# Handover from layer 0 to attention: last squares, row order of the first projection, evacuation, weight and key transfers

## The chip, the cores and the metric

The kernel runs on one core of one Trainium2 chip. The time is the device time of one execution in microseconds, and the figure for a kernel is the median of its runs. Before the change it is 2207.64 us (three runs, 2205.65 to 2208.02).

## What is computed

A trunk of two layers for one sequence of 1024 positions with 1024 features, all in float32. Layer 0 is a gated linear recurrence with a SwiGLU block behind it, layer 1 is stick-breaking attention (16 heads of 64) with a SwiGLU block of 2816 hidden features behind it; each block is normalised before and added to its input after. The change touches the end of layer 0's SwiGLU block and the attention:

```python
def swiglu_ffn(x, w_in, w_out):
    gu = jnp.einsum("bsd,df->bsf", x, w_in)
    h = jax.nn.silu(gu[..., :D_FF]) * gu[..., D_FF:]
    return jnp.einsum("bsf,fd->bsd", h, w_out)

# attention, per block of 128 queries
z = jnp.einsum("bhqd,bhkd->bhqk", qb, kb) * scale
log_fail = jnp.where(strict, jax.nn.log_sigmoid(-z), 0.0)
suffix = lax.cumsum(log_fail, axis=3, reverse=True) - log_fail
weights = jnp.where(strict, jnp.exp(jax.nn.log_sigmoid(z) + suffix), 0.0)
o = jnp.einsum("bhqk,bhkd->bhqd", weights, vb)      # then o @ w_o

# layers
h = h + mixer(rms_norm(h, mix_norm[layer]))
h = h + swiglu_ffn(rms_norm(h, ffn_norm[layer]), w_in, w_out)
```

## The kernel before

**Numbers and tiles.** Each float32 operand of a product is kept as two parts, a high part in a rounded format and the rest. A product is three matmuls, high by high, high by low, low by high (`mm3`, lines 140 to 143). Activations lie with features on partitions: `h[d][n]`, `xh[d][n]`, `xl[d][n]` for 8 feature tiles `d` and two halves `n` of 512 positions; `xh` and `xl` are the two parts of the next block's input (the trace names their memory `vh`, `vl` or `xg`). The norm's factor per position is applied behind a product: squares of the rows of `h` are summed in `rbc[n]`, `stats` (line 201) sums over partitions on PE, `rstd` (176 to 183) makes the factor on ACT and DVE, `broadcast_r` (189, 196) writes it back into `rbc[n]` over all partitions.

**The end of layer 0.** `mix_out_ffn_in` runs a SwiGLU block as seven products for eight (sums of weight and activation tiles, written to `wah`, `wal`, `wbh` and so on by ACT and DVE at lines 640 to 690). Its last part goes over 13 visits to pairs of output tiles (`VISITS`). When an output tile is final, `finished(d, n)` (1035) stores `h` on SP's queue, prepares `xh` on ACT (215) and `xl` on DVE (216), squares the tile on ACT (211) and adds the square to `rbc[n]` on DVE (212). The last two visits end the tiles 0, 3, 4 and 7.

**Attention.** `qkv_steps(q)` is a generator for the projections of one pair of heads `q` of eight. For queries, keys and values (`which` 0, 1, 2; one of these is called a link) and each half `n` it accumulates eight `mm3` into one of the two buffers of psQ, one per step, so a link has 16 steps. Behind the eighth, in the same step, it evacuates: DVE multiplies by `rbc[n]` into `t` (1337); for queries and keys ACT casts the high part (1346), DVE subtracts the low part (1347), and SP moves the parts to their places with four DMAs for queries and eight of 128 KB for keys (1348). Values go through four transposes on PE (1362) into another psQ buffer, a cast on ACT (1366) and a subtraction on DVE (1367) for each head; this is put off (`late`) until the fourth step of the next half, or to the end. The list `later` holds the low parts of the next link's weights (1309); their high part is one ACT cast at the start of the link (1307), which also asks for the raw weights (512 KB, three buffers).

**The order in attention** is written by hand for PE, ACT, DVE and POOL; a scheduler places SP's DMAs. First come 32 steps of the first pair, queries and keys, with the two statistics and broadcasts between them. Then one iteration per unit `u` from -8 to 191 (a head has 12 units): the scores of unit `u+8` (`z_part`, 1388 and 1389), transposes and split of the weights of unit `u+2` (`t_part` 1426, `t_split` 1435 and 1436), the rest of `u+8` (two sigmoids on ACT 1408 and 1409, a scan on DVE 1412 or 1414, a multiplication on POOL 1415), one item of `later`, two steps of `all_fill`, and the products with the values of unit `u` (`av_part`, 1447 and 1448). Outputs of finished heads are gathered and split (1457 to 1467), and most of them are stored to DRAM (`od`).

**The end of the projections.** `all_fill` takes the steps of all pairs, brings the stored outputs back into `xh` and `xl` with 26 DMAs of 256 KB (1495, 1496), waits two steps, transposes the last values, closes psQ, splits a weight of the output projection (168, 169), opens the PSUM tile `ob` in psQ's banks, waits two steps, and then does 14 `mm3` of the output projection into `ob`, one per unit.

Of the kernel before, what the change touches and what calls it, by code (L numbers as in the profile page):

```python
# [16 lines left out]
P = 128  # L17
S = 1024
# [15 lines left out]
def trunk(  # L34
# [92 lines left out]
    def cols(w, c0, n=P):  # L127
        return w[:, c0 : c0 + n].rearrange("(k p) c -> p k c", p=P)
# [468 lines left out]
    def mix_out_ffn_in(h, mix, bias, layer, gnext, ob):  # L597
# [124 lines left out]
        with tc.manual_schedule(engines={E.PE, E.Activation, E.DVE, E.Pool}):  # L722
# [309 lines left out]
            begun_sq = set()  # L1032
# [252 lines left out]
    with ExitStack() as st:  # L1285
# [11 lines left out]
        Q, KH, KL, VV = {}, {}, {}, {}  # L1297
# [5 lines left out]
        late, later = [], []  # L1303
# [11 lines left out]
        def qkv_steps(q):  # L1315
            full = lambda tag: [ap.tile([P, S], F32R, tag=tag, name=tag, bufs=4) for _ in range(2)]
            VV[q] = ap.tile([P, NT, 2, P], F32R, tag="v", name="v", bufs=2)
            for which in range(3):
                w = wq.pop((q, which))
                nx = (q, which + 1) if which < 2 else (q + 1, 0)  # L1320
                if nx[0] < NP:
                    wq[nx] = next_weights(load_raw(cols(w_qkv, nx[1] * D + nx[0] * P), (ND,)))
                else:
                    mix[0].load(0)
                    mix[0].w[mix[0].order[0]] = next_weights(mix[0].raw.pop(0))
                    mix[0].load(1)
                    mix[0].load(2)
                for n in range(NH):
                    ps = psQ.tile([P, NB], F32, tag="qk", name="qk_ps")
                    for k in range(ND):  # L1330
                        mm3(ps, w[0][:, k], w[1][:, k], xh[k][n], xl[k][n], k == 0, k == ND - 1)
                        if k == 3 and late:
                            late.pop()()
                        if k < ND - 1:
                            yield
                    t = ap.tile([P, NB], F32, tag="t", name="t", bufs=2)
                    nc.vector.tensor_mul(t, ps, rbc[n])
                    cs = slice(n * NB, (n + 1) * NB)
                    if which == 0 and n == 0:
                        Q[q] = full("q")  # L1340
                    if which == 1 and n == 0:
                        KH[q], KL[q] = full("kh"), full("kl")
                    if which < 2:
                        th = ap.tile([P, NB], F32R, tag="qh_", name="qh_", bufs=1)
                        tl = ap.tile([P, NB], F32R, tag="ql_", name="ql_", bufs=1)
                        nc.scalar.copy(th, t)
                        nc.vector.tensor_sub(tl, t, f32(th))
                        move = lambda dst, p0, src, p1: nc.sync.dma_start(f32(dst)[p0, cs], f32(src)[p1])
                        for hx, (a, b) in enumerate(((top, bot), (bot, top))):
                            if which == 0:  # L1350
                                move(Q[q][hx], a, th, a)
                                move(Q[q][hx], b, tl, a)
                            else:
                                for dst, src in ((KH[q][hx], th), (KL[q][hx], tl)):
                                    move(dst, top, src, a)
                                    move(dst, bot, src, a)
                    else:

                        def v_turn(n=n, t=t):
                            tp = psQ.tile([P, NB], F32, tag="qk", name="vt_ps")  # L1360
                            for i in range(4):
                                nc.tensor.transpose(tp[:, i * P : (i + 1) * P], t[:, i * P : (i + 1) * P], ident)
                            src = tp.rearrange("p (b h c) -> p b h c", b=4, h=2)
                            bs = slice(4 * n, 4 * n + 4)
                            for hx in range(2):
                                nc.scalar.copy(VV[q][:, bs, hx, 0:HD], src[:, :, hx])
                                nc.vector.tensor_sub(
                                    VV[q][:, bs, hx, HD:P], src[:, :, hx], f32(VV[q])[:, bs, hx, 0:HD]
                                )

                        late.append(v_turn)
                    yield
# [11 lines left out]
        def z_part(q, hx, j, ci, c0, c1, diag):  # L1384
            nk = (j + 1) * P
            ps = psZ.tile([P, NB], F32, tag="z", name="z_ps")
            lhsT = Q[q][hx][:, j * P : (j + 1) * P]
            nc.tensor.matmul(ps[:, 0 : c1 - c0], lhsT=lhsT, rhs=KH[q][hx][:, c0:c1], start=True, stop=False)  # L1388
            nc.tensor.matmul(ps[:, 0 : c1 - c0], lhsT=lhsT, rhs=KL[q][hx][:, c0:c1], start=False, stop=True)  # L1389
            return ps  # L1390
# [90 lines left out]

        def stats_steps():
            for n in range(NH):
                stats(rbc[n], psO, "o", n)
                for _ in range(ND - (1 if n else 6)):
                    yield
                broadcast_r(psO, "o", n)
                yield

        def all_fill():  # L1490
# [14 lines left out]
            for _ in range(2):  # L1505
                yield
# [85 lines left out]
```

## Time and profile before

| what | value |
|---|---|
| median of the runs | 2207.64 us |
| profiled execution | 2209.81 us |
| its span, first to last instruction | 2207.9 us |
| mean granted clock of PE | 0.994 |
| busy share of PE, DVE, ACT, POOL | 99%, 77%, 52%, 13% |
| layer 0 ends, projections begin | about 964 us |
| first scores, last projections | 994.3 us, 1431.6 us |

The profile gives the busy time of each engine, groups of instructions by line, the waits of an engine (how long it was idle before a line's instruction, and which instruction on which engine ended the idle time), and rows of single instructions: start, duration, engine, line, operation, what is written from what, and in brackets the idle time ahead of it with its releaser. Rows of a stretch give its limits, its length, the busy time of PE, of PE's weight load, DVE, ACT and POOL with their counts, the granted clock, and the share of the DMA engines. A clock under 1.00 makes the matmuls of the stretch longer, and the longer matmuls count as busy. Two matmuls overlap: the distance between their starts is what one costs.

### The profile page before, as it was taken

What the parts mean: (1) busy time and instruction counts of PE and PEld (TensorE: products, weight loads), DVE (VectorE), ACT (ScalarE), POOL (GpSimd) and SP (SyncE); (2) the same over time, 40 slices, a digit from 0 to 9 for tenths busy, and PEclk for the clock granted to TensorE, in tenths of its full rate; (3) what the DMA queues carried; (4) which work ended last, traced back from release to release, by engine and by line L of the source; (5) the groups of instructions that cost most, each with busy time, mean ns of one, the idle gap of its engine ahead of it and who ended that gap; (6) DMA issues with size and microseconds to landing.
All of it is one profiled execution on the core that took longest, in us unless ns stands there. A gap on an engine that the chain in (4) does not pass through costs nothing.

```text
span 2207.9 us, 28478 instructions
## 1 busy us (share of the span) xinstructions
PE 2176.5 (99%) x10120; PEld 1805.7 (82%) x10120; DVE 1709.9 (77%) x2383; ACT 1150.2 (52%) x2007; POOL 287.2 (13%) x379
## 2 busy tenths in 40 slices
PE   7999999999999999999999999989999999999998
PEld 6888888888888888878888888878888888888887
DVE  6887778767777887878888888876876777788876
ACT  5577435343444544546666666653533444454556
POOL 2222020000000000003334333321000000000002
PEclk9999999999999999999999999989999999999999
DMA  7111412334444764444333333532133444467442
GB/s 230 48 48 39 134 39 72 102 123 158 143 149 134 261 209 122 148 136 98 89 94 96 105 87 104 177 128 70 39 110 124 148 148 133 154 225 234 137 152 86
DMA packets 298702, 277.72 MB, mean 126 GB/s; under 512 B 16312, under 2 KB 215104, under 8 KB 298560
## 3 DMA queue, kind: packets, MB, share of 16 engines
q1 hardware_dynamic: 298544, 275.91, 40.1%
q8 instruction: 79, 1.29, 0.2%
q14 instruction: 63, 0.52, 0.1%
q10 hardware_dynamic: 16, 0.00, 0.0%
HBM read 175.71 MB, written 74.97 MB: 114 GB/s over the span
## 4 chain that ended last, share of the span: by engine, by line
PE 88%; DVE 6%; ACT 3%; DMA 1%; issue 1%; SPq 1%; DVEq 0%; ACTq 0%
PE p_ps L143 18%; PE p_ps L141 18%; PE p_ps L142 18%; PE qk_ps L143 3%; PE qk_ps L141 3%; PE qk_ps L142 3%; PE wt_ps L1426 3%; PE ob_ps L142 2%; PE ob_ps L141 2%; PE ob_ps L143 2%; PE a_ps L143 2%; PE a_ps L142 2%; PE a_ps L141 2%; PE z_ps L1388 1%; DVE F L1414 1%; PE z_ps L1389 1%
## 5 line engine op out<-in xcount | busy, mean ns | idle before, releaser
L1415 POOL TENSOR_TENSOR w<-w,F 128x128 f32<-128x128 f32 (+1 forms) x192 | 183.7, 957 | 311.1 <-DVE F L1412 159.0
L143 PE MATMUL p_ps<-vh,wcl 128*128 128x512 f32 x524 | 204.2, 390 | 0.5 <-DVE wcl L682 0.5
L143 PE MATMUL p_ps<-vh,wbl 128*128 128x512 f32 x524 | 204.4, 390 | 0.3 <-DVE wbl L672 0.2
L143 PE MATMUL p_ps<-vh,wal 128*128 128x512 f32 x524 | 204.1, 389 | 0.1
L141 PE MATMUL p_ps<-vh,wbh 128*128 128x512 f32 x524 | 204.2, 390 | 0.0
L141 PE MATMUL p_ps<-vh,wch 128*128 128x512 f32 x524 | 204.1, 389 | 0.0
L142 PE MATMUL p_ps<-vl,wbh 128*128 128x512 f32 x524 | 203.9, 389 | 0.0
L142 PE MATMUL p_ps<-vl,wch 128*128 128x512 f32 x524 | 203.9, 389 | 0.0
L141 PE MATMUL p_ps<-vh,wah 128*128 128x512 f32 x524 | 203.9, 389 | 0.0
L142 PE MATMUL p_ps<-vl,wah 128*128 128x512 f32 x524 | 203.9, 389 | 0.0
L668 ACT CAST wbh<-sb 128x1024 fp32r<-128x1024 f32 (+2 forms) x69 | 69.6, 1009 | 193.7 <-DVE sb L652 193.6
L212 POOL TENSOR_TENSOR acc<-acc,rbc 128x512 f32<-128x512 f32 x30 | 40.4, 1348 | 773.6 <-ACT rbc L211 773.6
L1436 DVE TENSOR_TENSOR tl<-wt_ps,th 128x512 fp32r<-128x512 f32 x192 | 106.0, 552 | 39.2 <-ACT th L1435 37.1
L1435 ACT CAST th<-wt_ps 128x512 fp32r<-128x512 f32 x192 | 92.5, 482 | 83.1 <-PE wt_ps L1426 82.0
L141 PE MATMUL qk_ps<-vh,whi 128*128 128x512 f32 x264 | 118.6, 449 | 0.7 <-ACT vh L215 0.7
L143 PEld LDWEIGHTS p_ps<-vh,wbl 128*128 128x128 f32 x524 | 98.3, 188 | 22.3 <-DVE wbl L672 2.0
L143 PEld LDWEIGHTS p_ps<-vh,wcl 128*128 128x128 f32 x524 | 98.4, 188 | 21.9 <-DVE wcl L682 1.6
L143 PEld LDWEIGHTS p_ps<-vh,wal 128*128 128x128 f32 x524 | 98.4, 188 | 21.3 <-DVE wal L663 1.0
L142 PEld LDWEIGHTS p_ps<-vl,wah 128*128 128x128 f32 x524 | 98.4, 188 | 20.6
L142 PEld LDWEIGHTS p_ps<-vl,wch 128*128 128x128 f32 x524 | 98.4, 188 | 20.5
L142 PEld LDWEIGHTS p_ps<-vl,wbh 128*128 128x128 f32 x524 | 98.4, 188 | 20.5
L141 PEld LDWEIGHTS p_ps<-vh,wbh 128*128 128x128 f32 x524 | 98.4, 188 | 20.3 <-ACT ta L1053 0.2
(400 smaller groups left out, 5851.2 us busy)
## 6 DMA issues: line engine op xcount, KB each, us to landing
raw<-in_ffn_w_in SPq DMA_DIRECT2D x88, 512.0 KB, 3.8
vl<-pd SPq DMA_DIRECT2D x128, 256.0 KB, 3.6
pd<-U SPq DMA_DIRECT2D x90, 256.0 KB, 2.3
raw<-in_ffn_w_out SPq DMA_DIRECT2D x56, 256.0 KB, 3.9
raw<-in_attn_w_qkv SPq DMA_DIRECT2D x24, 512.0 KB, 3.8
raw<-in_lru_w_in SPq DMA_DIRECT2D x16, 512.0 KB, 4.1
acc<-pd SPq DMA_DIRECT2D x28, 256.0 KB, 2.6
pph<-rbc SPq DMA_DIRECT2D x28, 256.0 KB, 2.5
```

The source lines that it names most:

```text
L141: nc.tensor.matmul(ps, lhsT=wh, rhs=mh, start=first, stop=False, **kw)
L142: nc.tensor.matmul(ps, lhsT=wh, rhs=ml, start=False, stop=False, **kw)
L143: nc.tensor.matmul(ps, lhsT=wl, rhs=mh, start=False, stop=last, **kw)
L212: (eng or nc.gpsimd).tensor_add(acc[n], acc[n], sq)
L668: nc.scalar.copy(self.full(self.wb), self.full(self.sb))
L1388: nc.tensor.matmul(ps[:, 0 : c1 - c0], lhsT=lhsT, rhs=KH[q][hx][:, c0:c1], start=True, stop=False)
L1389: nc.tensor.matmul(ps[:, 0 : c1 - c0], lhsT=lhsT, rhs=KL[q][hx][:, c0:c1], start=False, stop=True)
L1414: nc.vector.tensor_tensor_scan(rev, rev, rev, first, op0=ALU.mult, op1=ALU.bypass)
L1415: nc.gpsimd.tensor_mul(wt, wt, F[:, 1 : n + 1])
L1426: nc.tensor.transpose(tp[:, c : c + P], W[q, hx, j, kb // 4][:, (kb % 4) * P : (kb % 4 + 1) * P], ident)
L1435: nc.scalar.copy(th[:, q0:], tp[:, q0:])
L1436: nc.vector.tensor_sub(tl[:, q0:], tp[:, q0:], f32(th)[:, q0:])
```

## The change

1. `finished` no longer squares the tiles of the last two visits. Behind all products, eight pairs of a square on ACT and an addition on DVE follow, first half 0, then half 1, with two buffers in turn.
2. The first accumulations (pair 0, queries) read the feature tiles in the order 1, 5, 2, 6, 3, 7, 0, 4. Their two evacuations are kept in `waiting`; statistics, broadcasts and these evacuations stand at written places among 34 first steps instead of 32.
3. `evacuate` is a generator: the multiplication stands in the last step of a half, the cast, the subtraction and the DMAs in the next one.
4. Raw weights are asked for one link sooner (`load_link`). The high part is cast in two halves, and the items of `later` are: first half cast; first half subtracted and second half cast; second half subtracted.
5. High and low parts of queries or keys share one tile `two` with a single buffer. The keys' parts lie in one tile `kk`, and four DMAs of 256 KB replace eight.
6. The first 12 DMAs that bring outputs back are issued at the last value link's first half, the rest at the end of the projections. The two waiting steps ahead of the products into `ob` are gone. SP's order is written by hand too.

```diff
             def finished(d, n):
...
-                    squares(h, d, n, acc, rbc, V, first=n not in begun_sq)
+                    if d in (VISITS[-1][0], VISITS[-2][0], VISITS[-1][0] + HK, VISITS[-2][0] + HK):
+                        last_sq.append((d, n))
+                    else:
+                        squares(h, d, n, acc, rbc, V, first=n not in begun_sq)
...
+            last_sq.sort(key=lambda t: t[1])
+            for k, (d, n) in enumerate(last_sq):
+                nc.scalar.square(acc[k % NH], h[d][n])
+                V.tensor_add(rbc[n], rbc[n], acc[k % NH])
...
+        def bring_back(*which):
+            for q, n in which:
+                nc.sync.dma_start(f32(xh[q][n]), od[q, n][0])
+                nc.sync.dma_start(f32(xl[q][n]), od[q, n][1])
+        def load_link(i):
+            q, which = divmod(i, 3)
+            if q < NP:
+                raws[i] = load_raw(cols(w_qkv, which * D + q * P), (ND,))
+            else:
+                mix[0].load(which)
...
-            nc.scalar.copy(hi, raw)
-            for i in range(NH):
-                later.append(lambda c=half(hi, i), a=half(lo, i), b=half(raw, i): nc.vector.tensor_sub(a, b, f32(c)))
+            part_hi = lambda i: nc.scalar.copy(half(hi, i), half(raw, i))
+            part_lo = lambda i: nc.vector.tensor_sub(half(lo, i), half(raw, i), f32(half(hi, i)))
+            def second():
+                part_lo(0)
+                part_hi(1)
+            later.extend((lambda: part_hi(0), second, lambda: part_lo(1)))
...
         def qkv_steps(q):
...
-                if nx[0] < NP:
-                    wq[nx] = next_weights(load_raw(cols(w_qkv, nx[1] * D + nx[0] * P), (ND,)))
+                if at < 3 * NP:
+                    wq[divmod(at, 3)] = next_weights(raws.pop(at))
...
+                for i in (at + 1,) if at < 3 * NP else (at + 1, at + 2):
+                    load_link(i)
+                ks = (1, 5, 2, 6, 3, 7, 0, 4) if (q, which) == (0, 0) else range(ND)
...
+                    ev = evacuate(q, which, n, ps)
+                    if (q, which) == (0, 0):
+                        waiting.append(ev)
+                        yield
                     else:
+                        next(ev)
+                        yield
+                        next(ev, None)
+        def evacuate(q, which, n, ps):
...
+            t = ap.tile([P, NB], F32, tag="t", name="t", bufs=2)
+            nc.vector.tensor_mul(t, ps, rbc[n])
+            yield
...
+            if which < 2:
+                two = ap.tile([P, 2, NB], F32R, tag="two", name="two", bufs=1)
+                nc.scalar.copy(two[:, 0], t)
+                nc.vector.tensor_sub(two[:, 1], t, f32(two)[:, 0])
+                for hx, (a, b) in enumerate(((top, bot), (bot, top))):
+                    if which == 0:
+                        nc.sync.dma_start(f32(Q[q][hx])[a, cs], f32(two)[a, 0])
+                        nc.sync.dma_start(f32(Q[q][hx])[b, cs], f32(two)[a, 1])
+                    else:
+                        for half_ in (top, bot):
+                            nc.sync.dma_start(f32(KK[q][hx])[half_, :, cs], f32(two)[a])
+                return
...
+            late.append(v_turn)
+            if q == NP - 1 and n == 0:
+                bring_back(*((p, 0) for p in range(NP - 2)))
...
         def all_fill():
...
-            for q, n in od:
-                nc.sync.dma_start(f32(xh[q][n]), od[q, n][0])
-                nc.sync.dma_start(f32(xl[q][n]), od[q, n][1])
+            bring_back((NP - 2, 0), *((p, 1) for p in range(NP - 2)))
             yield
             yield
             late.pop()()
...
-            for _ in range(2):
-                yield
...
-        with tc.manual_schedule(engines={E.PE, E.Activation, E.DVE, E.Pool}):
-            sts, first = stats_steps(), qkv_steps(0)
-            for i in range(2 * ND * NH):
-                if i >= 5:
-                    next(sts, None)
+        with tc.manual_schedule(engines={E.PE, E.Activation, E.DVE, E.Pool, E.SP}):
+            load_link(1)
+            first = qkv_steps(0)
+            between = {
+                11: lambda: stats(rbc[0], psO, "o", 0),
+                15: lambda: stats(rbc[1], psO, "o", 1),
+                16: lambda: broadcast_r(psO, "o", 0),
+                17: lambda: [*waiting[0]],
+                20: lambda: broadcast_r(psO, "o", 1),
+                21: lambda: [*waiting[1]],
+            }
+            for i in range(1, 2 * ND * NH + 3):
                 next(first)
-                if i >= 5 and later:
+                if i in between:
+                    between[i]()
+                if i > 4 and later:
                     later.pop(0)()
```

More of the change, by code (lines that the diff above doesn't have):

```diff
@@ L1315, in qkv_steps @@
         def qkv_steps(q):
-            full = lambda tag: [ap.tile([P, S], F32R, tag=tag, name=tag, bufs=4) for _ in range(2)]
-            VV[q] = ap.tile([P, NT, 2, P], F32R, tag="v", name="v", bufs=2)
             for which in range(3):
-                w = wq.pop((q, which))
-                nx = (q, which + 1) if which < 2 else (q + 1, 0)
-                if nx[0] < NP:
-                    wq[nx] = next_weights(load_raw(cols(w_qkv, nx[1] * D + nx[0] * P), (ND,)))
+                w, at = wq.pop((q, which)), 3 * q + which + 1
@@ L1335, in qkv_steps @@
                             yield
[L1336 to L1356, printed above, removed]
-                    else:
[L1359 to L1371, printed above, removed]
@@ L1372, in qkv_steps, with v_turn @@
-                    yield
+                    ev = evacuate(q, which, n, ps)
+                    if (q, which) == (0, 0):
+                        waiting.append(ev)
+                        yield
+                    else:
+                        next(ev)
+                        yield
+                        next(ev, None)
+        def evacuate(q, which, n, ps):
+            full = lambda tag, m: [ap.tile([P, m, S], F32R, tag=tag, name=tag, bufs=4) for _ in range(2)]
+            t = ap.tile([P, NB], F32, tag="t", name="t", bufs=2)
+            nc.vector.tensor_mul(t, ps, rbc[n])
+            yield
+            cs = slice(n * NB, (n + 1) * NB)
+            if which == 0 and n == 0:
+                Q[q] = [t[:, 0] for t in full("q", 1)]
+            if which == 1 and n == 0:
+                KK[q] = full("kk", 2)
+            if which < 2:
[10 more added lines that the diff above has]
+                return
+            if n == 0:
+                VV[q] = ap.tile([P, NT, 2, P], F32R, tag="v", name="v", bufs=2)
+            def v_turn():
+                tp = psQ.tile([P, NB], F32, tag="qk", name="vt_ps")
+                for i in range(4):
+                    nc.tensor.transpose(tp[:, i * P : (i + 1) * P], t[:, i * P : (i + 1) * P], ident)
+                src = tp.rearrange("p (b h c) -> p b h c", b=4, h=2)
+                bs = slice(4 * n, 4 * n + 4)
+                for hx in range(2):
+                    nc.scalar.copy(VV[q][:, bs, hx, 0:HD], src[:, :, hx])
+                    nc.vector.tensor_sub(VV[q][:, bs, hx, HD:P], src[:, :, hx], f32(VV[q])[:, bs, hx, 0:HD])
+            late.append(v_turn)
+            if q == NP - 1 and n == 0:
+                bring_back(*((p, 0) for p in range(NP - 2)))
```

29 lines of the change are left out of this document (9 added, 20 removed).

## The prediction

> **What bounds the kernel now.** The page's first part comes first, then the list of TensorE's (PE's) waits.
>
> ```profile
> PE 2176.5 (99%) x10120; PEld 1805.7 (82%) x10120; DVE 1709.9 (77%) x2383; ACT 1150.2 (52%) x2007; POOL 287.2 (13%) x379
> ```
> ```profile
> PE ob L141 <- issue: 3.9, 1, 3.9
> PE wt_ps L1426 <- DVE tl L1436: 2.7, 2, 1.6
> PE z_ps L1388 <- ACT w L1409: 2.5, 7, 0.4
> ...
> PE qk_ps L141 <- ACT vh L215: 0.7, 1, 0.7
> PE p_ps L143 <- DVE wcl L682: 0.5, 1, 0.5
> PE p_ps L141 <- ACT ta L1053: 0.4, 1, 0.4
> ```
>
> PE is busy 2176.5 of 2207.9 us, and the change leaves its matmuls as they are. So all that can be won is idle time of PE, 31.4 us in the whole span, and time at a lower granted clock, which counts as busy. The rows of the waits say where the change can reach idle time: the last three are the passage from the products of layer 0 to the first projection (place A, 956 to 999 us), the third is one small wait in each pair of heads (place S), the first is the end of the projections (place B, 1436 us), the second the units after it (place C). The table by stretches (length, busy time of PE, PEld, DVE, ACT, POOL, granted clock) adds what the clock takes:
>
> ```profile
> 948.00:960.00 12.00, 11.39 (x49) 8.65 (x48) 11.90 (x23) 8.12 (x16) 0.00 (x0) 1.00 0.50 163
> 968.00:972.00 4.00, 2.68 (x13) 1.94 (x13) 2.65 (x5) 2.56 (x5) 0.69 (x3) 0.92 0.58 198
> 972.00:976.00 4.00, 4.00 (x17) 3.33 (x17) 2.44 (x8) 0.17 (x1) 0.00 (x0) 0.66 0.07 13
> 1100.00:1150.00 50.00, 49.63 (x265) 41.59 (x264) 42.50 (x62) 33.25 (x83) 19.82 (x31) 1.00 0.39 106
> 1440.00:1448.00 8.00, 8.00 (x31) 6.77 (x32) 6.46 (x9) 5.17 (x16) 2.62 (x5) 0.64 0.50 140
> ```
>
> Between the places PE runs at its rate (49.63 of 50). At A the idle time of 968 to 972 is followed by a clock of 0.66; lost are (1 - 0.92) x 4 + (1 - 0.66) x 4 = 1.7 us. At B 0.64 of 8 us loses 0.36 x 8 = 2.9 us. DVE is full ahead of A (11.90 of 12), so A begins as DVE's place.
>
> **The change part by part.** *A, squares and row order.* Eight squares on ACT and eight additions on DVE go behind the last products.
>
> ```profile
> L211 ACT ACTIVATE acc<-h 128x512 f32<-128x512 f32 x8 | 5.0, 621 | 0.7 <-DVE rbc L212 0.7
> ```
> ```profile
> L212 DVE TENSOR_TENSOR rbc<-rbc,acc x14: 681/684/685, 926.2 to 969.8; 128x512 f32<-128x512 f32 x14
> ```
>
> That takes 8 x 0.68 = 5.5 us out of the full DVE and 5.0 us out of ACT ahead of the handover; and because the projection reads the tiles of the last products (0, 4) as its seventh and eighth, 20 matmuls instead of 11 lie between the last product and the tile that is prepared last. I take the waits of the products and of the projection as gone, and with them the lower clock. What is late next follows from rows of this place:
>
> ```profile
> 967.73 0.39 PE L143 MATMUL qk_ps<-xg,wlo 128*128 128x512 f32 x1
> 968.77 0.51 PE L141 MATMUL qk_ps<-vh,whi 128*128 128x512 f32 x1 [0.66 <-ACT vh L215]
> 969.95 0.50 PE L142 MATMUL qk_ps<-vl,whi 128*128 128x512 f32 x1 [0.67 <-DVE vl L216]
> ...
> 974.30 1.27 PE L189 MATMUL rb_ps<-ident,rcol 128*128 128x128 f32 x8
> ```
> ```profile
> 976.38 0.69 DVE L1337 TENSOR_TENSOR t<-qk_ps,rbc 128x512 f32<-128x512 f32 x1
> ...
> 989.04 0.69 DVE L1337 TENSOR_TENSOR t<-qk_ps,rbc 128x512 f32<-128x512 f32 x1 [1.69 <-PE qk_ps L143]
> ```
> ```profile
> 985.11 0.69 DVE L1347 TENSOR_TENSOR ql__7675<-t,qh__7674 128x512 fp32r<-128x512 f32 x1 [0.73 <-ACT qh__7674 L1346]
> ```
> ```profile
> 986.97 0.59 SPq L1348 DMA_DIRECT2D q<-ql__7675  x1
> ```
> ```profile
> 995.97 0.62 ACT L1346 CAST qh__7759<-t 128x512 fp32r<-128x512 f32 x1 [5.53 <-DMA kh<-qh__7720]
> ```
> ```profile
> 986.12 0.39 PE L141 MATMUL qk_ps<-vh,whi 128*128 128x512 f32 x1
> ...
> 994.06 0.39 PE L143 MATMUL qk_ps<-vh,wlo 128*128 128x512 f32 x1
> 994.28 0.28 PE L1388 MATMUL z_ps<-kh,q 128*128 128x256 f32 x1
> ...
> 998.40 0.44 PE L1388 MATMUL z_ps<-kh,q 128*128 128x384 f32 x1 [0.32 <-ACT w L1409]
> ```
> ```profile
> kh<-qh__7720 SPq DMA_DIRECT2D x4, 128.0 KB, 2.3
> ...
> q<-ql__7619 SPq DMA_DIRECT2D x2, 128.0 KB, 2.9
> ```
>
> A matmul takes (994.06 - 986.12) / 35 = 0.227 us, a step of three 0.68. Start to start the waits that go cost more than their idle time: 968.77 - 967.73 - 0.23 = 0.81 for 0.66, so 0.8 + 0.9 here and by the same 0.7 + 0.6 for `wcl` and `ta`; with the 1.7 of the clock and the slow small groups of statistics PE comes some 5.5 us sooner (estimate). The eight pairs of squares run at some 0.7 us each, so the first statistics find their sums, and the second wait some 0.5 us for the eighth. The first broadcast then starts at about 976.4. New is that the third accumulation (loop step 17) needs a bank of psQ (two buffers) that only the held-back evacuation frees. From the broadcast's start to the end of that multiplication were 976.38 + 0.69 - 974.30 = 2.8 us; 0.81 of it is the broadcast itself and the rest PE's wait, **1.8 to 2.0 us** (estimate). Queued behind it are all PE's matmuls. The second broadcast comes four steps behind this wait, at about 981.9, and by the same rows the second evacuation multiplies to about 984.3 and is split at 985.8. The first half of the keys ends at about 985.2, eight steps and a broadcast behind the wait; its multiplication, now at 989.04, comes some 4 us sooner. Here the one buffer of the tile `two` decides: its next cast waits until all four DMAs of the queries have landed. The last is issued at about 986.9, as now (986.97); landed after 2.4, between the 2.3 and 2.9 of the rows, at 989.3; cast and subtraction take 0.73 + 0.69 as in the row at 985.11, so the keys are split at 990.7. From there to the scores the present run shows at most 994.28 - (989.04 + 0.69 + 0.73 + 0.69) = 3.1 us; I take 3.5 for the larger transfers. The first scores start at **994.2**, as now (994.28), where PE is ready at some 994.28 - 5.5 + 0.5 + 1.9 + 2 x 0.68 = 992.5. Then the second half's cast waits for these DMAs, and on ACT it and two half casts of weights stand ahead of the table load and the first sigmoids, where now only the row at 995.97 does: the third scores come at some 998.75, now 998.40. Against that PE has done 34 steps, not 32, ahead of the first scores, 1.36 us more. A brings 998.75 - 998.40 - 1.36 = **-1.0 us**.
>
> The ends: by landings of 2.3 us the scores wait for nothing, the third come at 996.6, and A brings -3.2; by the 5.5 between two casts that the row at 995.97 shows, eight issues and a landing, the first scores come some 3 us later, and A costs +2.0.
>
> What the new waits do to the clock is open. At 968 to 972 an idle 1.32 us, in two parts, went ahead of the lower clock. By that, each of the two new waits, of about 2 us, may be followed by it, at up to 1.7 us each; the sum takes none, the range one.
>
> [...]
>
> *S, evacuation a step later.* The wait is seen best in one pair.
>
> ```profile
> 1083.70 0.62 ACT L1346 CAST qh__8813<-t 128x512 fp32r<-128x512 f32 x1 [3.28 <-DVE t L1337]
> ```
> ```profile
> 1084.99 0.44 PE L1388 MATMUL z_ps<-kh,q 128*128 128x384 f32 x1 [0.37 <-ACT w L1409]
> ```
>
> ACT has been idle for 3.28 us with the query's cast at the head of its queue, because DVE comes late to `t`; behind it stand the next unit's copy and sigmoids, for which PE waits. After the change the cast stands behind those sigmoids. Of the seven waits (2.5 us) the 0.32 at 998.40 lies in A; six are here, one per pair: 2.5 - 0.3 = **-2.2 us**. Nothing replaces them: cast and subtraction keep their work, and DVE, busy 42.50 of 50 us, has room. If the cover failed (the multiplication later than a whole unit), the same waits would stay, so 0 is the other end.
>
> *Weights a link ahead, in half casts; keys in pairs.* A cast becomes two halves on an engine that is at 33.25 of 50 us: nothing. The raw tiles are asked for a link of 16 steps sooner, into three buffers; PE never waited for them. 64 fewer DMAs on SP gain nothing, since no wait of PE in this stage has a transfer behind it. SP now goes in program order; what could block it is a key DMA that waits for its subtraction, at most a step. Bounds for these together: -0.5 to +1.0, value 0.
>
> *B, last transfers sooner and two steps fewer.* What does the wait of 3.9 us end with?
>
> ```profile
> 1439.27 0.42 DVE L1367 TENSOR_TENSOR v<-vt_ps,v 128x256 fp32r<-128x256 f32 x1 [0.44 <-ACT v L1366]
> ```
> ```profile
> 1439.80 0.76 PE L141 MATMUL ob<-vh,whi 128*128 128x512 f32 x1 [3.91 <-issue]
> ```
>
> The last subtraction of v ends at 1439.69, and 0.11 later the first product into `ob` starts, in the banks that this subtraction has read. It is not the returning tiles. So the earlier transfers bring nothing here. The product now stands right behind the transposes, a unit sooner; PE reaches it about 1.1 us sooner (a unit's products, scores and transposes stand behind it), while DVE's order between `t` and that subtraction loses one scan and two subtractions and gains one scan and one subtraction, some 0.5 to 0.8 us. So the wait grows a little, and the low clock behind it stays: **+0.3**, ends -0.6 and +0.8 (estimates).
>
> *C.* Both shifts let the 14 products end two units sooner: two units more run without them.
>
> ```profile
> 1470.60 1.33 PE L1426 MATMUL wt_ps<-ident,w 128*128 128x128 f32 x4 [1.62 <-DVE tl L1436]
> ```
>
> There PE already waits for DVE's scans. If the units 182 and 183 wait too, two products (1.36 us) that lay in a wait no longer do; if not, nothing. I take the middle, **+0.7**.
>
> Sum: -1.0 - 2.2 + 0 + 0.3 + 0.7 = **-2.2 us**. The profiled execution took 2209.8 us (span 2207.9 and 1.9 around it) and would take 2207.6; it stood 2.2 above the median of the runs, 2207.64. So 2207.64 - 2.2 = 2205.4 us.
>
> **The rivals.** *R1, the wait at B is one for transfers.* Then sending them sooner ends it and the clock stays up: -3.9 - 2.9 = -6.8 in place of +0.3, 2198.3 us. For it speaks that the profile names no engine as releaser ("issue"); against it the 0.11 us between subtraction and product. *R2, the queries land fast.* With A at -3.2 the sum is -4.4: 2203.2 us; landings of 2.3 us, as the row of the keys has, decide. *R3, slower: the single `two` becomes a chain.* Queries' landing, cast, keys' landing, cast stand in a row, with no second buffer, ahead of the first scores. It decides once the landings exceed the 2.4 and 3.5 us taken here by more than about 1 us together. Two landings at 5.5 us cost 3.1 + 2.0, and PE's wait, longer than that of B, is followed by a low clock as there, 2.9: -2.2 + 8.0 = +5.8, 2213.4 us. Against it: the q rows show 2.9. *R4, the later half-step does nothing.* If the cast in S still comes ahead of the sigmoids, +2.2: 2207.6 us.
>
> **How the numbers follow.** Chances: forecast 0.50, R1 0.12, R2 0.16, R3 0.14, R4 0.08. The range reaches from R1's end to between R4 and R3: 2198.5 to 2211.5; the forecast's own is 2203 to 2209 by the bounds of A and C and one drop of the clock. A measurement can tell 0.2%, 4.4 us: faster is below 2203.2, slower above 2212.1. Faster takes R1, half of R2 and the lower tenth of the forecast and a little for places that I have not seen: 0.30. Slower is R3 and little else: 0.15. Within: 0.55.
>
> **What would show it.** A: no row `p_ps <- wcl`, `ta` or `qk_ps <- vl`, `vh` among PE's waits, a new one of about 2 us at the accumulation behind the first broadcast and one at the first scores; clock 1.00 from 968 to 976. S: no wait of z_ps for w between 1000 and 1430. B: `ob` still starts within 0.2 us of v's last subtraction, 0.50 behind it. The forecast is wrong if B's wait is gone (R1), if the first scores wait for over 4 us (R3), or if idle time turns up between 1000 and 1430.

## The result and the profile after

The changed kernel takes **2213.95 us** (median of 7 runs, 2212.90 to 2215.38) against 2207.64 before on the same chip: a ratio of 1.0031, with a 95% interval of 1.0019 to 1.0043. It is slower by 6.3 us; 2.2 us faster was forecast, and the time lies above the range. The profiled execution took 2213.4 us (span 2211.6), 3.6 more than that of before, which lay above all seven runs of its kernel.

The waits of TensorE in the changed kernel, in the columns of the prediction's list (total, times, longest):

```profile
PE ob L141 <- issue: 5.2, 1, 5.2
...
PE wt_ps L1461 <- DVE tl L1471: 3.4, 3, 1.3
PE z_ps L1423 <- issue: 3.1, 1, 3.1
PE av_ps L1482 <- DVE oo L1493: 2.5, 6, 0.7
...
PE qk_ps L141 <- DVE t L1373: 1.5, 1, 1.5
...
PE z_ps L1423 <- ACT w L1444: 0.9, 1, 0.9
...
PE st_ps L201 <- DVE rbc L1206: 0.3, 1, 0.3
```

The waits that the prediction named as lost are gone: no `qk_ps <- vh`, no `vl`, no `wcl`, no `ta`, and the scores no longer wait once per pair for `w`. But six waits of `av_ps` for `oo`, 2.5 us, stand where the six waits of `z_ps` stood, 2.2 us: as many, and as long. Idle time between 1000 and 1430 is what the prediction had named as a sign of being wrong. And the handover has two new waits for the scores, 3.1 and 0.9 us, beside the 1.5 of the third accumulation.

Where the time went is read from marks, each but the last the start of the same matmul in both traces:

| mark | before | after | difference | from the first mark on | forecast |
|---|---|---|---|---|---|
| a product of layer 0, ahead of the change | 881.22 | 880.40 | -0.82 | 0 | 0 |
| third scores | 998.40 | 1000.72 | +2.32 | +3.14 | +0.35 |
| scores of unit 166 | 1407.32 | 1410.75 | +3.43 | +4.25 | -1.85 |
| last product with the values (high part) | 1478.06 | 1481.79 | +3.73 | +4.55 | -2.2 |
| end of the span | 2207.9 | 2211.6 | +3.7 | +4.5 | -2.2 |

Up to the first mark TensorE does the same matmuls in the same order, yet over all the traces of this case that product starts anywhere from 879.14 to 881.23, a spread that arises nearly all in the first 50 us. So two traces are compared from this mark on:

```profile
881.22 0.39 PE L141 MATMUL p_ps<-vh,wd 128*128 128x512 f32 x1
```
```profile
880.40 0.39 PE L141 MATMUL p_ps<-vh,wd 128*128 128x512 f32 x1
```

The handover (place A) was to cost 0.35 with two steps more done, and costs 3.1. Between it and unit 166 (place S) 2.2 us were to go, and 1.1 came on top. The end of the projections and the tail (B and C) took 0.3 more in place of 0.35 less. The two steps done sooner do show there: 54 matmuls of projections lie in this stretch instead of 60. But the waits in it grew from 6.6 to 8.9 us, by more than the 1.36 us of the steps. The rest is as before. So two places failed, A by 2.8 us and S by 3.3.

At A, first ScalarE's rows of the changed kernel, then TensorE's, then the stretch:

```profile
988.95 0.62 ACT L1382 CAST two<-t 128x512 fp32r<-128x512 f32 x1 [4.34 <-DMA q<-two]
997.25 0.62 ACT L1382 CAST two<-t 128x512 fp32r<-128x512 f32 x1 [7.67 <-DMA kk<-two]
997.77 1.14 ACT L1328 CAST whi<-raw 128x512 fp32r<-128x512 f32 x2
998.93 1.28 ACT L1443 ACT_TABLE_LOAD   x1
1000.22 0.28 ACT L1443 ACTIVATE F<-z_ps 128x128 f32<-128x128 f32 x1
```
```profile
995.11 0.55 PE L1423 MATMUL z_ps<-kk,q 128*128 128x256 f32 x1 [3.08 <-issue]
...
1000.72 0.44 PE L1423 MATMUL z_ps<-kk,q 128*128 128x384 f32 x1 [0.86 <-ACT w L1444]
```
```profile
992.00:1000.00 8.00, 4.77 (x17) 3.66 (x16) 1.29 (x2) 2.74 (x4) 0.00 (x0) 0.79 0.53 124
```
```profile
kk<-two SPq DMA_DIRECT2D x8, 256.0 KB, 4.2
q<-two SPq DMA_DIRECT2D x8, 128.0 KB, 2.3
```

The first cast of keys comes at 988.95, when the queries have landed; 989.3 was forecast, and counted from the first mark the cast is 0.5 us later than that. The second cast comes 8.3 us later, because the four key transfers of 256 KB (4.2 us to landing in the median, the 128-KB ones 2.3) hold the only `two`. Between 992 and 1000 PE is busy 4.77 of 8 us, and at a clock of 0.79.

At S, one pair of the changed kernel, VectorE and TensorE:

```profile
1082.89 1.27 DVE L1449 TENSOR_TENSOR_SCAN F<-F,F 128x512 f32<-128x512 f32 x1
1084.20 0.69 DVE L1493 TENSOR_TENSOR oo<-av_ps,oo 64x512 f32<-64x512 f32 x1
```
```profile
1084.95 0.50 PE L1482 MATMUL av_ps<-th,v 128*128 128x512 f32 x1 [0.38 <-DVE oo L1493]
```

The product with the values begins a new group in one of psO's two banks, and that bank is read by the gathering of the group before the last, at 1084.20. In the kernel before, the same gathering came 8.7 us ahead of that product:

```profile
1073.19 0.69 DVE L1458 TENSOR_TENSOR oo<-av_ps,oo 64x512 f32<-64x512 f32 x1
```
```profile
1081.92 0.39 PE L1447 MATMUL av_ps<-th,v 128*128 128x512 f32 x1
```

### The profile page after: what moved, and what is told of

Same layout as the page of the kernel before. It is cut to its first block, busy times and chain, and to the rows that moved or that the text cites. A ratio compares the mean times of both kernels' runs of the same rounds, so it can differ in the third digit from the quotient of the medians.

```text
span 2211.6 us, 28421 instructions
## 1 busy us (share of the span) xinstructions
PE 2175.8 (98%) x10120; PEld 1805.0 (82%) x10120; DVE 1706.3 (77%) x2383; ACT 1155.6 (52%) x2031; POOL 295.2 (13%) x379
## 4 chain that ended last, share of the span: by engine, by line
PE 91%; DVE 4%; ACT 2%; DMA 1%; issue 1%; SPq 1%; POOL 0%; DVEq 0%; ACTq 0%; POOLq 0%
PE p_ps L143 18%; PE p_ps L141 18%; PE p_ps L142 18%; PE qk_ps L143 3%; PE qk_ps L141 3%; PE qk_ps L142 3%; PE wt_ps L1461 3%; PE ob_ps L142 2%; PE ob_ps L141 2%; PE ob_ps L143 2%; PE a_ps L143 2%; PE a_ps L141 2%; PE a_ps L142 2%; PE z_ps L1423 2%; PE av_ps L1482 2%; PE z_ps L1424 1%
## 5 line engine op out<-in xcount | busy, mean ns | idle before, releaser
L1450 POOL TENSOR_TENSOR w<-w,F 128x128 f32<-128x128 f32 (+1 forms) x192 | 191.7, 998 | 304.4 <-DVE F L1447 187.7
L141 PEld LDWEIGHTS p_ps<-vh,wch 128*128 128x128 f32 x524 | 98.4, 188 | 20.4 <-ACT tb L1057 0.2
```

The lines of the kernel that those rows point to most:

```text
L141: nc.tensor.matmul(ps, lhsT=wh, rhs=mh, start=first, stop=False, **kw)
L1450: nc.gpsimd.tensor_mul(wt, wt, F[:, 1 : n + 1])
```

## The experiments

All times are medians of device time; each run was timed beside the kernel before on its chip, whose medians were 2207.46 to 2207.72. A period is a fifth of the time from the scores of unit 40 to those of unit 160, so one pair: 60.40 us before ((1392.11 - 1090.10) / 5), 60.60 in the changed kernel ((1395.50 - 1092.50) / 5).

**e1_later2: two put-off items per link, not three.**

```diff
-            later.extend((lambda: part_hi(0), second, lambda: part_lo(1)))
+            part_hi(0)
+            later.extend((second, lambda: part_lo(1)))
```

> The changed kernel, but each link of weights puts two items into the list of put-off work instead of three: the first half of the high part is cast at the start of the link. Theory 1: the third item delays the gathering of a finished head by one unit, so that the next group's product with the values finds its PSUM buffer still unread; that is the wait of 0.38 us once per pair. Then the six waits of the products for oo are gone, the period of a pair falls from 60.54 to about 60.0 us, and the time lies 3 us below the changed kernel's 2213.95, at about 2211. Rival 1: the later subtraction of the evacuation is what makes DVE late, and the waits stay (2214).

Measured: 2209.97 us (2208.34 to 2211.29; ratio to before 1.0009, interval 1.0000 to 1.0018), 4.0 below the changed kernel. The waits between 1000 and 1430 us, the stretch without the handover, and the handover's stretch, all of this run:

```profile
PE z_ps L1424 <- ACT w L1445: 2.2, 1, 2.2
```
```profile
1050.00:1400.00 350.00, 350.00 (x1874) 295.36 (x1873) 300.47 (x435) 234.52 (x584) 150.86 (x235) 1.00 0.37 97
```
```profile
992.00:1000.00 8.00, 3.60 (x17) 2.65 (x16) 1.90 (x3) 2.59 (x4) 0.00 (x0) 1.00 0.54 124
```

The six waits for `oo` are gone and PE is busy 350.00 of 350; the period is 59.94. The gathering now comes at 1081.82, 2.7 us ahead of its product (1084.55). So the third item in the list was what made the gathering too late, and the later subtraction was not. The one wait left is at A. There the third scores come at 1000.86, as in the changed kernel, though the clock is 1.00 here and was 0.79 there (the first mark lies at 880.44 and 880.40): the low clock is not what sets them.

**e2_split: high and low parts in two tiles, keys by eight transfers.**

```diff
-                two = ap.tile([P, 2, NB], F32R, tag="two", name="two", bufs=1)
-                nc.scalar.copy(two[:, 0], t)
-                nc.vector.tensor_sub(two[:, 1], t, f32(two)[:, 0])
+                th = ap.tile([P, NB], F32R, tag="qh_", name="qh_", bufs=1)
+                tl = ap.tile([P, NB], F32R, tag="ql_", name="ql_", bufs=1)
+                nc.scalar.copy(th, t)
+                nc.vector.tensor_sub(tl, t, f32(th))
...
-                        for half_ in (top, bot):
-                            nc.sync.dma_start(f32(KK[q][hx])[half_, :, cs], f32(two)[a])
+                        for part, src in enumerate((th, tl)):
+                            for half_ in (top, bot):
+                                nc.sync.dma_start(f32(KK[q][hx])[half_, part, cs], f32(src)[a])
```

> The changed kernel, but with high and low parts of queries and keys in two tiles again and the keys moved by eight transfers of 128 KB. Theory 2: the chain of the one tile and the 256-KB transfers (4.2 to 4.8 us to landing, where the 128-KB ones took 2.3) sets the first scores; then the keys' first cast comes at about 988.2 instead of 988.95 and the second at about 994.4 instead of 997.25, the first scores at about 993.6 instead of 995.11, and the time lies 1.5 to 3 us below 2213.95, at about 2211.5. Rival 2: the transfers are slow at this place whatever their size; then cast and scores stay within 0.5 us and so does the time.

Measured: 2210.20 us (2208.84 to 2213.52; ratio 1.0011, 1.0003 to 1.0020), 3.8 below the changed kernel. ScalarE and TensorE of this run:

```profile
987.92 0.62 ACT L1383 CAST qh__7721<-t 128x512 fp32r<-128x512 f32 x1 [3.67 <-DMA q<-qh__7700]
994.06 0.62 ACT L1383 CAST qh__7760<-t 128x512 fp32r<-128x512 f32 x1 [5.52 <-DMA kk<-qh__7721]
```
```profile
997.53 0.44 PE L1425 MATMUL z_ps<-kk,q 128*128 128x384 f32 x1 [1.32 <-ACT w L1446]
```

Both casts come within 0.4 us of where theory 2 put them (988.2 and 994.4), and the third scores at 997.53, 3.2 us sooner, or 2.7 counted from the first mark (879.95 here). The period stays at 60.54, so this cost is apart from that of S.

**e3_keys8: one tile, eight transfers.**

```diff
-                            nc.sync.dma_start(f32(KK[q][hx])[half_, :, cs], f32(two)[a])
+                            for part in range(2):
+                                nc.sync.dma_start(f32(KK[q][hx])[half_, part, cs], f32(two)[a, part])
```

> The changed kernel with the one tile, but the keys moved by eight transfers of 128 KB. It parts size from coupling. If the landing of a 256-KB transfer is the cost, the second cast comes some 2 us sooner than 997.25; if issue time on SP's queue makes up for it (eight issues at 0.6 us, the cast waits for all eight), the second cast stays within 1 us of 997.25 and the first scores come within 0.5 us of 995.1. I expect the second.

Measured once: 2215.98 us; only its trace is used. The second cast and the third scores of this run:

```profile
996.68 0.62 ACT L1382 CAST two<-t 128x512 fp32r<-128x512 f32 x1 [6.93 <-DMA kk<-two]
```
```profile
1000.14 0.44 PE L1424 MATMUL z_ps<-kk,q 128*128 128x384 f32 x1 [2.65 <-ACT w L1445]
```

The second cast moves by 0.6 us and the third scores by 0.6; the first scores, which wait for half of the transfers, come at 993.62, 1.5 sooner, more than expected. So the small transfers freed the tile hardly sooner: eight issues, at about 0.6 us each, took what the shorter landing gave. It is the coupling of both parts in one tile with one buffer that costs, in which e2 differs from this run (and in the order of its eight transfers). A second buffer for `two`, the plainest test, was not run.

**e4_rest_only: the kernel before, with the later rest alone, from the second pair on.**

```diff
                     nc.vector.tensor_mul(t, ps, rbc[n])
+                    if q and which < 2:
+                        yield
...
-                    yield
+                    if not q or which == 2:
+                        yield
```

> The kernel before, with one part of the change: from the second pair on, cast, subtraction and transfers of queries and keys stand in the step behind the multiplication. The prediction's step S: the six waits of the scores for the sigmoids go and nothing replaces them, -2.2 us, 2205.4. Rival: DVE's later subtraction delays the gathering of a head and the product with the values waits instead; then the period of a pair stays at 60.4 us and the time within 1 us of 2207.6.

Measured: **2202.26 us** (2200.15 to 2204.13; ratio 0.9973, 0.9961 to 0.9984), 5.2 below before: faster than forecast for this part by more than two. The waits from 1000 to 1430 and a stretch of this run:

```profile
PE z_ps L1391 <- ACT w L1412: 0.3, 1, 0.3
```
```profile
1050.00:1400.00 350.00, 350.00 (x1883) 297.04 (x1882) 301.80 (x437) 236.54 (x568) 149.34 (x237) 1.00 0.36 97
```

The period is 59.63, 0.78 less than before, where the wait's idle time was 0.37. In the trace of before the matmuls around that wait show the rest:

```profile
1084.28 0.34 PE L1448 MATMUL av_ps<-tl,v 128*128 128x384 f32 x1
...
1085.27 0.34 PE L1389 MATMUL z_ps<-kl,q 128*128 128x384 f32 x1
1085.53 0.63 PE L1426 MATMUL wt_ps<-ident,w 128*128 128x128 f32 x4
```

From the product ahead of it to the waiting one (1084.99) are 0.71 us, where products of this width start 0.17 apart; the next two starts, 0.28 and 0.26 apart, are late by 0.11 and 0.09: 0.74 in all. In e4 the same four start 0.18, 0.17 and 0.18 apart. The one wait that is left lies at A (1000.04).

**e5_later2_split and e6_whole_split.** The first has the edits of e1 and e2. The second has those of e2, and casts the weights whole again (so two put-off items):

```diff
-            later.extend((lambda: part_hi(0), second, lambda: part_lo(1)))
+            nc.scalar.copy(hi, raw)
+            for i in range(NH):
+                later.append(lambda c=half(hi, i), a=half(lo, i), b=half(raw, i): nc.vector.tensor_sub(a, b, f32(c)))
```

> The changed kernel with both edits of the first two experiments: two items of put-off weight work per link, and high and low parts in two tiles with eight key transfers. Theory: the late gathering (place S) and the key chain (place A) are two separate costs, so they add: 4.0 + 3.8 us below 2213.95, about 2206.2, with a period of 59.9 us and the third scores at about 997.5. Rival: both feed the same stretch, so that the second brings less; then about 2209.

> The run above, but with the high part of the weights cast whole at the start of the link, as before the change, and only the two subtractions put off. The first run with two items had a period of 59.94 us, the kernel before with the later rest alone 59.63. If the half casts are what is left, the period falls to 59.6 and the time by some 1.8 us to about 2204.5; if not, it stays at 59.9 and 2206.

Measured: 2207.12 us (2205.55 to 2208.94; ratio 0.9998, 0.9989 to 1.0007) and 2206.47 (0.9999, 0.9990 to 1.0008). The two costs add up nearly in full, 6.8 of 7.7 us. The periods are 59.93 and 59.94, so the half casts are not what parts them from e4's 59.63.

**e7_yields: the two waiting steps ahead of `ob` put back.**

```diff
             mix.append(ob)
+            for _ in range(2):
+                yield
```

> The changed kernel with the two waiting steps ahead of the products into ob put back. By the prediction's step B and C the wait of 5.2 us shrinks to about 3.9 and one unit more of the tail is covered, while the products start later: within 1 us of 2213.95. Rival: without the two steps the tail stands open for DVE, and putting them back brings over 2 us.

Measured: 2211.08 us (2209.92 to 2212.51; ratio 1.0018, 1.0009 to 1.0027), 2.9 below the changed kernel. The wait falls to 4.2 us:

```profile
PE ob L141 <- issue: 4.2, 1, 4.2
```

The rival is nearer in the size. One part of it is the 1.0 us of wait; the rest may be the low clock behind it, as the stretches of the changed kernel and of this run show:

```profile
1432.00:1448.00 16.00, 10.77 (x48) 8.57 (x47) 11.42 (x15) 9.02 (x23) 3.78 (x5) 0.79 0.90 313
```
```profile
1432.00:1448.00 16.00, 11.80 (x59) 9.66 (x59) 13.88 (x18) 11.06 (x29) 5.52 (x6) 0.89 0.92 307
```

The granted clocks of all runs point the same way: their mean is 0.9954 in the changed kernel and 0.9960 here, some 1.3 us of 2210 (estimate). The two weren't told apart by an experiment of their own.

**e8_squares_at_once: the squares as before.** `finished` squares every tile at once again; row order and all else stay.

> The changed kernel, but the squares of the last two visits are made at once, as before; row order and all else stay. By the prediction DVE is then full again ahead of the handover: the waits of the products for wcl and ta come back (about 0.5 and 0.4 idle, 1.3 us from start to start), the first projection begins up to 2.9 us later (960.89 now, 963.75 before), and as the keys' chain hangs on it the third scores come 1 to 2.5 us later: 2215 to 2216.5. Rival: the chain of the key transfers hides all of it, and the time stays within 0.5 us.

Measured: 2214.05 us (2212.95 to 2214.52; ratio 1.0029, 1.0018 to 1.0041), no difference to the changed kernel. Waits of this run from 940 to 1000 us:

```profile
PE z_ps L1423 <- issue: 3.2, 1, 3.2
PE qk_ps L141 <- DVE t L1373: 1.5, 1, 1.5
PE p_ps L143 <- DVE wcl L682: 0.5, 1, 0.5
PE p_ps L141 <- ACT ta L1057: 0.4, 1, 0.4
```

The two waits of the products come back as expected and the projection begins 1.4 us later (962.27 against 960.89), the third scores 0.5 (1001.22). Counted from the first mark (879.74 here) it is 2.0 and 1.2 us, so the third scores are late by as much as expected, and the key chain hides only the rest. The time, all the same, is the rival's: the put-off squares work and bring nothing measurable here.

**e9_parts123, e10_parts123_kk and e12_parts123_32.** e9 has parts 1 to 3 of the change alone; weights, keys, transfers back, waiting steps and SP's order are those of before. e10 is e9 with the joint tile `kk`. e12 is e9 with 32 first steps:

```diff
-            for i in range(1, 2 * ND * NH + 3):
+            for i in range(1, 2 * ND * NH + 1):
```

> The first three parts of the change alone: last squares behind the products, row order with 34 first steps, evacuation's rest a step later. Weights, keys, transfers back, waiting steps and SP's order are as before the change. The run with the later rest alone took 2202.26 with the third scores at 1000.04; the changed kernel with split tiles had them at 997.5 with two more steps done (1.36 us). Theory: the handover's gain is real once the key chain is short, so 2202.3 - 2.5 - 1.4 = about 2198.5, and the period of a pair is 59.63. Rival: the period is 59.93, because the shift of the steps by one unit, not the tiles or the transfers, makes products with the values and scores slower; then about 2200.5.

> The run above with the keys' high and low parts in one tile kk of two rows, still written by eight transfers from two tiles. If the joint tile is what makes scores and products some 5 ns longer each (59.93 us per pair against 59.63), the time is 2 us above the run above; if not, equal within 1 us.

> The run with parts one to three alone, but with 32 first steps as before the change instead of 34, so that the projection's steps stand in the units where they stood before. Theory: the shift by one unit costs 0.31 us per pair (59.93 against 59.63), so the period comes back to 59.63 and the time falls by some 2 to 4 us, to 2202 to 2203.5, at or a little below the later rest alone (2202.26). Rival: the period stays at 59.93 and the time at 2205 or above, because something else of the three parts (order of put-off work, memory places) makes the products slower.

Measured: e9 2205.74 us (2203.75 to 2206.61; ratio 0.9989, 0.9980 to 0.9998), e10 2205.66 (0.9989, 0.9980 to 0.9998), e12 2203.55 (2200.13 to 2205.52; 0.9982, 0.9973 to 0.9991). Periods: 59.93, 59.93, 59.63. The rival of e9 holds in the period, not in the time, which lies 5 us above its 2200.5: that sum compared third scores of e4 and e2 whose first marks lie 1.3 us apart. The 34 steps put every step of the projection one unit sooner, and that alone costs 0.31 us per pair; the joint tile costs nothing. The matmuls of scores and values of e9, then of e12, from 1050 to 1400 us (busy time, mean ns):

```profile
L1478 PE MATMUL av_ps<-th,v 128*128 128x512 f32 x71 | 29.0, 408 | 0.0
...
L1420 PE MATMUL z_ps<-kl,q 128*128 128x512 f32 x69 | 27.5, 399 | 0.0
L1419 PE MATMUL z_ps<-kh,q 128*128 128x512 f32 x69 | 27.2, 395 | 0.0
```
```profile
L1478 PE MATMUL av_ps<-th,v 128*128 128x512 f32 x71 | 28.4, 400 | 0.0
...
L1420 PE MATMUL z_ps<-kl,q 128*128 128x512 f32 x70 | 27.5, 393 | 0.0
L1419 PE MATMUL z_ps<-kh,q 128*128 128x512 f32 x70 | 27.2, 389 | 0.0
```

Each lasts 6 to 8 ns longer in e9, without a wait. What they meet in the other unit's place isn't known. The shift also changes the order of the put-off work: in e12 the gathering comes at 1070.86, 8.7 us ahead of its product as in the kernel before, in e9 at 1079.32, behind the two items of a link and 2.7 us ahead. e12 is faster than before, but not faster than e4 (the intervals overlap), although its third scores come at 996.31 and those of e4 at 1000.04. These 3.7 us are no measure of the handover: 1.0 lies ahead of the first mark (880.21 and 881.23), PE's clock from 972 to 976 was 0.50 in the trace of e4 and 1.00 in that of e12, and the one is the slowest of its kernel's runs, the other the fastest.

**e11_mended_yields: the edits of e1, e2 and e7 together.**

> The changed kernel with three mends: two put-off items per link, split tiles with eight key transfers, the two waiting steps back. The first two together gave 2207.12, the third alone 2.9 us less than the changed kernel. If they add: 2204.2. If the third one's gain was a matter of where the low clock fell, about 2206.

Measured: 2205.71 us (2204.05 to 2206.91; ratio 0.9992, 0.9982 to 1.0001), 8.2 below the changed kernel and 1.4 below e5. The third mend adds about half of its 2.9 us; the case of the low clock is the nearer one. The mean clocks of e5 and e11 are alike (0.9963 and 0.9964), so the 1.4 us here go without the clock's share, and the wait alone is 1.0 of them.

## Why the prediction was wrong

*A, squares and row order: right.* Four waits went, the clock is 1.00 from 968 to 976, the second statistics waited 0.28 us (0.5 forecast), the third accumulation 1.51 (1.8 to 2.0), and the queries had landed within 0.5 us of the forecast.

*A, the chain of `two`: the mechanism was right, the sizes were not.* The sum took 3.5 us from the split keys to the first scores; measured are 995.11 - (989.61 + 0.69) = 4.8, with 4.2 us for the landing of a transfer of 256 KB from 64 partitions. I had priced it by the present 3.1, which was an upper bound for the small transfers and none for large ones. The third scores then hang on the second cast, which waits for all four: they come 5.6 us behind the first, where the forecast had 4.55 (998.75 - 994.2). So R3's mechanism came true, at its point of decision (1.3 us over the figures taken), but cost 2.8 us more than forecast and not 8.0: the low clock (0.79 from 992 to 1000) lay beside the wait, as e1 shows. The 2.8 are 0.5 up to the first cast, 1.3 of the landing and 1.0 behind the first scores. With it A turned from -1.0 to +1.8 (3.14 - 1.36). e2 takes it away. R2 falls with the 4.2 us. That R3's 2213.4 us lie near the measured time is luck: half of the miss is at S, which R3 doesn't touch.

*S, the wait of the scores: half its size.* The step "2.5 - 0.3 = -2.2 us" counted idle time. In A the prediction had reckoned that a wait costs more from start to start; in S it didn't. The later rest alone is worth 0.78 us per pair, and the kernel that has only it is 5.2 us faster (e4), so R4 falls.

*S, "Nothing replaces them": wrong, and one of the two large costs.* The sentence that failed stands one part further: half casts "nothing" on an engine with room. Room was not the cost. The half casts make three put-off items per link out of two; the list gives out one item per unit, in order, and the gathering of a finished head stands in the same list. With 34 first steps a link starts one unit sooner, and its items then stand ahead of the gathering instead of behind it, which leaves 2.7 us of the 8.7 (e9, e12); the third item takes one unit more, and the gathering is too late for psO's two banks. e1 removes the third item: -4.0 us. Mended at S or at A alone the kernel stays some 2.5 us above before (e1, e2); the two together bring it level (e5).

*Nothing for the shift by one unit: wrong.* 34 first steps were booked as 1.36 us of work done sooner. Every later step then stands one unit sooner, and each pair takes 0.31 us longer, some 2 us over the projections (e9 and e12). The three terms of S add up per pair: -0.78 for the rest, +0.66 for the third item, +0.31 for the shift are +0.19, and the period grew by 0.20. The 1.36 us are there at the end, as six matmuls fewer, but the longer waits of B and C take them.

*B: right in its cause.* In the changed kernel the last subtraction of v, then the first product:

```profile
1440.45 0.42 DVE L1403 TENSOR_TENSOR v<-vt_ps,v 128x256 fp32r<-128x256 f32 x1 [0.44 <-ACT v L1402]
```
```profile
1440.97 0.77 PE L141 MATMUL ob<-vh,whi 128*128 128x512 f32 x1 [5.23 <-issue]
```

0.10 us lie between them, as 0.11 before, though the transfers back were issued sooner: R1 falls. The wait grew by 1.3 us, not a little as forecast, and one scan in DVE's chain took longer than the 1.2 to 1.4 us of the scans of its width around it and at this place before:

```profile
1436.72 2.11 DVE L1449 TENSOR_TENSOR_SCAN F<-F,F 128x512 f32<-128x512 f32 x1
```

*C.* Its waits grew by 1.0 us, from 2.7 to 3.4 and 0.3 for POOL, where 0.7 was forecast. Together B and C came out 0.65 us worse than forecast; the mean clock of that stretch is 0.90 in both traces, and e7 and e11 leave the clock's share open.

*From the profile to the median.* The profiles differ by 3.6 us, by 4.5 from the first mark on, and the medians by 6.3. The prediction subtracted its sum from the median; the profiled execution of before was simply 2.2 above its kernel's median, and its start alone took 0.8 longer than in the trace after. Within one kernel the runs spread over 2 to 5 us.

The mends account for the loss: 2213.95 less 8.2 is 2205.71 (e11), about the forecast time, but by another way than the forecast's. The best measured is the one part alone, e4.

## What to carry to other kernels

A queue of put-off work that gives out one item per step is a schedule: an item added to it can cost nothing on its engine and still delays all behind it (4.0 us of the time here, e1), and a shift of the work that fills it can change its order, so ask which items have a due time. Where several transfers left from one tile with one buffer, the tile was free when the last had landed, and what waited for it was a chain of landings (8.3 us between the two casts of keys here). Before marks of two traces are subtracted, look whether they agree ahead of the change. Try the parts of a bundle one by one: one of six was worth 5 us here, and the others took away more.

## What the runs showed of the hardware

A transfer of 256 KB out of 64 partitions took 4.2 us from issue to landing (median) where 128 KB out of 64 partitions took 2.3, and eight of these, at about 0.6 us of issue each, freed the tile only 0.6 us sooner than four of those.

An idle time of TensorE of 3.08 us ahead of the first scores was followed by a lower clock in the changed kernel (0.79 from 992 to 1000). In e1 about 3.1 us stood there (an estimate from its rows: 8.00 less 3.60 busy from 992 to 1000, less the 1.3 us of that stretch that belong to the wait ahead of the third scores), and the clock was 1.00. In the kernel before, 1.3 us in two parts, from 968 to 972, were followed by 0.66 from 972 to 976; the 1.51 us ahead of the third accumulation of the changed kernel, which end at 978.56, were followed by 1.00 up to 984. So in these traces the length of a wait alone did not tell whether a lower clock came behind it, and what did was not shown.
